# First norm of a hybrid mLSTM / attention / MoE block: the transposes of x go tile of tokens by tile of tokens, and the rotary angles and lambda move into the second projection group

## The chip, the cores and the metric

The kernel runs on one core of a Trainium2 chip. The metric is the device time of one execution in microseconds (us). An engine executes its own instructions in the order in which the program issues them (the schedule is written out by hand, `tc.manual_schedule()`), and waits on semaphores where an operand comes from another engine. The names are those of the profile: PE is TensorE (PEld its weight loads), DVE is VectorE, ACT is ScalarE, POOL is GpSimd, SP is SyncE, which issues most of the DMAs.

## The reference

One decoder block on 512 tokens of width 1024, all in float32:

```python
h = rmsnorm(x, norm1_w) * (1.0 + scale1) + shift1          # scale1, shift1 from c @ w_ada + b_ada
proj = h @ w_in                                             # 5640 columns
(q_m, k_m, v_m, o_m, i_pre, f_pre, q_d, k_d, v_d, g_m, g_d) = split(proj)
qk = silu(causal_conv([q_m, k_m]));  hm = mlstm(...)        # mLSTM branch
qd, kd = partial_rope(rmsnorm(q_d), positions), partial_rope(rmsnorm(k_d), positions)
lam = exp(sum(lam_q1 * lam_k1)) - exp(sum(lam_q2 * lam_k2)) + lam_init
hd = diff_attention(qd, kd, vd, lam)                        # a = p0 - lam * p1
merged = sigmoid(g_m) * (hm @ w_br_m) + sigmoid(g_d) * (hd @ w_br_d)
x = x + gate1 * (merged @ w_out)
x = x + gate2 * hierarchical_moe(rmsnorm(x) * (1 + scale2) + shift2)   # 32 experts, top 2 of one group
```

The change touches the first norm with its modulation (scale1, shift1), the cosines and sines of `partial_rope`, and `lam`.

## The kernel before, in words

**The start.** x comes in four tiles of 128 tokens (`xu`, L115 to L118). For each tile ACT sums the squares (L222), POOL makes 1/rms (L223, L193) and DVE scales the tile in place (L225). The projections need x with the 1024 features on the partitions, so PE transposes 32 blocks of 128x128: `xT(j)` (L306) does feature block j for all four token tiles in one PSUM bank, and ACT (even j) or DVE (odd j) copies the bank back over x in two halves. `mod_rows(fb)` (L278) multiplies c by the part of `w_ada` that belongs to feature blocks 2fb and 2fb+1 (tiles `ada0[fb]`, 2 MB each), ACT copies the row out (L286), `mod_cols(fb)` (L288) turns the row into columns with four small matmuls, and DVE makes the factor and the addend `AB1` from them (L294 to L297). `hT_pair(fb)` (L317) then writes the modulated blocks as a high part (`hTh`, ACT) and a low part (`hTl`, DVE). `warm(n)` issues n matmuls whose result nobody reads.

Between the transposes stand the angles (L354 to L368: DVE, then a Sin on ACT), lambda's exponents (L372 to L374: DVE, then an Exp on ACT), the tables `ropet` (L382) and lambda itself (L384, L385), which one tiny matmul `lamp` (L394) spreads over the partitions and DVE copies to `nlam` (L395). `nlam` and the tables are read much later, by the attention and by `qk_prep`.

**The projections.** `pstream` (L424) runs groups of eight chunks. A chunk is 128 rows of `w_in` by 512 columns: ACT copies them to a high part (L407), DVE or POOL in turn makes the low part (L408), three chunks ahead of use (`LA = 3`), and PE does twelve matmuls of 512 columns (L457 to L459), for each of four banks high by high, high by low, low by high. Behind the chunk's matmuls the program issues what `at(g, k, f)` has put down for group g, chunk k. Then `run` (L478) takes up to two items from the queue `later` and one step of each side generator. In the first group (g = 0) `hT_next` does the modulation of the later feature blocks between the chunks. At its end four banks go out, and each puts a `conv` (L510) into `later`: one ACT instruction (L513), three DVE instructions (L517), and a Silu on ACT (L524) that is inserted behind the next conv. One conv is taken for each chunk, so the four convs fall behind the last chunk of the first group and the first three chunks of the second.

**The rest.** Nine more groups, in whose side generators mLSTM and attention run, then the branch and output projections, the routing, and 16 pairs of experts, whose weights are loaded into buffers as these come free.

The order of SP's DMAs at the start is: x, the four lambda vectors, `ada0[0]`, the first 1 MB of `w_in` (`P0a[0]`), the gate weights, `ada0[1]`, and then halves of `P0a[1]` in turn with `ada0[2]` and `ada0[3]`.

Of the kernel before, what the change touches and what calls it, by code (L numbers as in the profile page):

```python
# [10 lines left out]
F32 = mybir.dt.float32  # L11
# [22 lines left out]
R0, R1 = 3, 0  # L34
RT = (0, 0, 0, 0, 0)
REF = {4: 5, 7: 3, 11: 4}
W0 = (0, 2, 6)
EY, SY = 2, 0
W1 = 6
GF = False  # L40
# [17 lines left out]
def block_kernel(ctx, tc, x, c, positions, w_ada, b_ada, norm1_w, w_in, b_igate, b_fgate, conv_w, conv_b,  # L58
# [16 lines left out]
    def U(name, shape, dt=F32):  # L75
        return up.tile(shape, dt, name=name, tag="u")
# [13 lines left out]
    def ps2(name="ps2"):  # L90
        return ps.tile([128, 2, 512], F32, name=name, tag="s", bufs=1)
# [13 lines left out]
    mrow = dc.tile([24, 128], F32, name="mrow")  # L105
    G.dma_start(posi, positions[0].rearrange("(t p) -> t p", p=128))
    qkw16 = dc.tile([128, 2, 16], F32, name="qkw16")
    for i, w in enumerate((q_norm_w, k_norm_w)):
        G.dma_start(qkw16[:, i], bass.AP(tensor=w.tensor, offset=w.offset, ap=[[0, 128], [1, 16]]))
    cz = amc.rearrange("p a (k f) -> p (a k) f", f=32)  # L110
    S.dma_start(crow[0:8], c[0].rearrange("(j p) -> j p", p=128))
    S.dma_start(crow[8:16], norm1_w[0].rearrange("(j p) -> j p", p=128))
# [2 lines left out]
    xu = [U(f"x{a}", [128, 2, 1024]) for a in range(2)]  # L115
    for t in range(4):
        SP.dma_start(xu[t // 2][:, t % 2], x2[t * 128:(t + 1) * 128])
    for i, w in enumerate((lam_q1, lam_k1, lam_q2, lam_k2)):  # L118
        SP.dma_start(lamt[:, i], w)

    def ada_panel(ch, j):
        t = U("wada", [128, 2048])
# [28 lines left out]

    P0a, P0b = [], []
    load_ada0(0)
    load_unit(P0a, 0, 0, 512)
    SP.dma_start(wif_raw, win[:, 2048:2056].rearrange("(k p) f -> p k f", p=128))
    load_ada0(1)
    P0a.append(U("wp", [128, 4, 512]))
    for i in range(2):
        SP.dma_start(P0a[1][:, 2 * i:2 * i + 2], win[512 + i * 256:768 + i * 256, 0:512].rearrange("(k p) f -> p k f", p=128))
        load_ada0(i + 2)  # L160
    SP.dma_start(rows[0:32], conv_w[0].rearrange("w (j p) -> (w j) p", p=128))
    SP.dma_start(rows[32:40], conv_b[0].rearrange("(j p) -> j p", p=128))
    SP.dma_start(rows[40:44], mlstm_norm_w[0])
# [1 line left out]
    for m in range(2):  # L165
        SP.dma_start(rows[45:46, m * 64:(m + 1) * 64], q_norm_w)
        SP.dma_start(rows[46:47, m * 64:(m + 1) * 64], k_norm_w)

    gb = dc.tile([64, 1], F32, name="gb")
    SP.dma_start(gb[0:4], b_igate[0].rearrange("(h o) -> h o", o=1))  # L170
# [27 lines left out]
    V.memset(onesc, 1.0)  # L198
    onesb = onesc.to_broadcast([128, 128])

    V.tensor_copy(posf, posi)
    post = dc.tile([128, 4], F32, name="post")
    posp = pt("posp", (128, 4))
# [6 lines left out]
    colp = pt("colp", (128, 32))  # L210
    PE.transpose(colp, crow, ident[0:32, 0:32])
    V.tensor_copy(ccols, colp)
    G.memset(cz, 0.0)
    V.tensor_copy(cz[:, :, 0:1], ccol[:, :, None])

# [52 lines left out]
    st = {}  # L268
    AB1 = dc.tile([128, 2, 8], F32, name="AB1")


    def warm(n):
        if n:
            p = ps2("warm")[0:64, 0]
            for _ in range(n):
                PE.matmul(p, wi[:, 0, 0:64], wi[:, 0:4].rearrange("p k f -> p (k f)"), start=True, stop=True)

    def mod_rows(fb):  # L278

        modp = pt("modp") if fb else ps2("modp")[:, 0]  # L280
# [7 lines left out]
    def mod_cols(fb):  # L288

        modp, a_ = pt("modp"), st["ada1"]  # L290
        for i in range(4):
            PE.matmul(modp[:, i:i + 1], a_[:, i * 128:(i + 1) * 128], ones[:, 0:1], start=True, stop=True)
        sl = slice(fb * 2, fb * 2 + 2)
        V.tensor_add(AB1[:, 0, sl], modp[:, 0:2], bcol[:, sl])  # L294
        V.scalar_tensor_tensor(AB1[:, 1, sl], modp[:, 2:4], 1.0, bcol[:, fb * 2 + 8:fb * 2 + 10],
                               op0=ALU.add, op1=ALU.add)
        V.tensor_mul(AB1[:, 1, sl], AB1[:, 1, sl], n1col[:, sl])  # L297

    hTh = [U(f"hTh{a}", [128, 4, 512], F32R) for a in range(2)]
    hTl = [U(f"hTl{a}", [128, 4, 512], F32R) for a in range(2)]  # L300
# [2 lines left out]
    def xcol(j, a):  # L303
        return xu[a][:, :, j * 128:(j + 1) * 128]

    def xT(j):  # L306
        p = pt("xtp") if j in (4, 5) else acc("xtp")
        for t in range(4):
            PE.transpose(p[:, t * 128:(t + 1) * 128], xu[t // 2][:, t % 2, j * 128:(j + 1) * 128], ident)
        for a in range(2):  # L310
            d, q = xcol(j, a), p[:, a * 256:(a + 1) * 256].rearrange("p (t f) -> p t f", t=2)
            if j % 2:
                V.tensor_copy(d, q)
            else:
                S.activation(d, q, AF.Copy)

    def hT_pair(fb):  # L317
        fs = []
# [32 lines left out]
    kf = dc.tile([128, 4, 8], F32, name="kf")  # L351
    MAGIC = 12582912.0
    PI = 3.1415925
    for i in range(8):  # L354
        V.memset(invf[:, i:i + 1], INV_FREQ[i])
    xT(0)
    xT(1)
    V.tensor_mul(ang[:, 1], post[:, :, None].to_broadcast([128, 4, 8]), invf[:, None, :].to_broadcast([128, 4, 8]))
    V.tensor_scalar(kf, ang[:, 1], 1.0 / (2 * math.pi), MAGIC, op0=ALU.mult, op1=ALU.add)
    V.tensor_scalar(kf, kf, -MAGIC, None, op0=ALU.add)  # L360
    for cst in TWO_PI_PARTS:
        V.scalar_tensor_tensor(ang[:, 1], kf, -cst, ang[:, 1], op0=ALU.mult, op1=ALU.add)
    V.tensor_scalar(ang[:, 0], ang[:, 1], math.pi / 2, None, op0=ALU.add)
    V.tensor_scalar(kf, ang[:, 0], math.pi, -2 * math.pi, op0=ALU.is_gt, op1=ALU.mult)
    V.tensor_add(ang[:, 0], ang[:, 0], kf)
    V.tensor_scalar(ang, ang, -PI, PI, op0=ALU.max, op1=ALU.min)
    xT(2)
    S.activation(ang, ang, AF.Sin)  # L368
    xT(3)

    ls = dc.tile([1, 4], F32, name="ls")
    V.tensor_mul(lp, lamt[:, 0:4:2], lamt[:, 1:4:2])  # L372
    V.reduce_sum(ls[:, 0:2], lp, axis=AX.X)
    S.activation(ls[:, 0:2], ls[:, 0:2], AF.Exp)  # L374
    xT(4)
    xT(5)
    rope = []
    for i in range(2):
        tb = dc.tile([128, 4, 4, 8], F32, name=f"ropet{i}")

        for n, (cs, o_) in enumerate(((0, 0), (1, 8), (0, 8), (1, 0))):
            V.tensor_mul(tb[:, n], ang[:, cs], qkw16[:, i, None, o_:o_ + 8].to_broadcast([128, 4, 8]))  # L382
        rope.append(tb)
    V.tensor_sub(ls[:, 2:3], ls[:, 1:2], ls[:, 0:1])  # L384
    V.tensor_scalar(ls[:, 3:4], ls[:, 2:3], -(0.8 - 0.6 * math.exp(-0.3 * 0)), None, op0=ALU.add)  # L385
    warm(W0[0])
    mod_rows(0)
    xT(6)
    xT(7)
    warm(W0[1])  # L390
    mod_cols(0)
    nlam = const.tile([128, 1], F32, name="nlam")
    lamp = acc("lamp")
    PE.matmul(lamp[:, 0:1], ones[0:1, 0:1].to_broadcast([1, 128]), ls[:, 3:4], start=True, stop=True)  # L394
    V.tensor_copy(nlam, lamp[:, 0:1])  # L395
    warm(W0[2])
    pif = ps2("pif")[:, 0]


# [24 lines left out]
    def pstream(groups, ev=None):  # L424
        ev = ev or {}
        chunks = [(g, k) for g in groups for k in range(g.nk)]
        sp_of = {}
        nxt = 0
        for idx, (g, k) in enumerate(chunks):
            if k == 0 and g.pre:  # L430
                g.pre()
            while nxt < len(chunks) and nxt <= idx + LA:
                gg, kk = chunks[nxt]
                sp_of[nxt] = split(gg.w(kk))
                nxt += 1
                if nxt == 1 and g.after:
                    hT_pair(0)
                    wif_split()
            if k == 0:
                g.banks = [acc() for _ in range(4)]  # L440
            wh, wl = sp_of.pop(idx)
            ah, al = g.act(k)
            st, en = (k == 0), (k == g.nk - 1)
            for b in range(4):
                sl = slice(b * 128, (b + 1) * 128)
                if g.kind == "O":
                    hh, tl = b % 2, b // 2
# [1081 lines left out]
```

## Time and profile before

| | us |
|---|---|
| median of three runs | 715.04 (714.26 to 715.83) |
| the profiled execution | 714.36 |
| its span, first to last instruction | 712.6 |
| PE busy | 669.8 (94%) |
| DVE busy | 380.1 (53%) |
| ACT busy | 236.1 (33%) |
| POOL busy | 196.3 (28%) |
| mean granted PE clock | 0.992 |

The rows further down are from the profiled execution; their times count from the first instruction. A row of the timeline gives the start, the duration, engine, line, operation, output and inputs, and how many instructions of one kind are merged in it; in brackets stands how long the engine had been idle before, and what ended that.

### The profile page before, as it was taken

What the parts mean: (1) busy time and instruction counts of PE and PEld (TensorE: products, weight loads), DVE (VectorE), ACT (ScalarE), POOL (GpSimd) and SP (SyncE); (2) the same over time, 40 slices, a digit from 0 to 9 for tenths busy, and PEclk for the clock granted to TensorE, in tenths of its full rate; (3) what the DMA queues carried; (4) which work ended last, traced back from release to release, by engine and by line L of the source; (5) the groups of instructions that cost most, each with busy time, mean ns of one, the idle gap of its engine ahead of it and who ended that gap; (6) DMA issues with size and microseconds to landing.
All of it is one profiled execution on the core that took longest, in us unless ns stands there. A gap on an engine that the chain in (4) does not pass through costs nothing. (4 is left out here: it accounts for less than half of the span.)

```text
span 712.6 us, 11438 instructions
## 1 busy us (share of the span) xinstructions
PE 669.8 (94%) x4464; PEld 493.6 (69%) x4464; DVE 380.1 (53%) x765; ACT 236.1 (33%) x511; POOL 196.3 (28%) x204
## 2 busy tenths in 40 slices
PE   3999999999998999999999999699999999999972
PEld 2668887878777777778867888676667566766630
DVE  4746469866685467763795855763222332233211
ACT  5536582452443455542322234541111111111100
POOL 5213252436552213243253531121111121111100
PEclk9999999999999999999999999999999999999997
DMA  9973069215125011056636984779999999999971
GB/s 300 368 258 150 1 247 402 98 45 187 57 74 178 1 59 60 1 206 221 240 115 237 423 373 178 295 295 357 371 374 379 408 404 378 395 373 401 404 290 21
DMA packets 47386, 171.50 MB, mean 241 GB/s; under 512 B 8009, under 2 KB 16338, under 8 KB 32990
## 3 DMA queue, kind: packets, MB, share of 16 engines
q1 hardware_dynamic: 44510, 165.41, 60.2%
q0 software_dynamic: 2752, 5.28, 3.8%
q8 instruction: 37, 0.61, 0.3%
q14 instruction: 23, 0.19, 0.1%
q10 hardware_dynamic: 64, 0.02, 0.0%
HBM read 164.37 MB, written 10.51 MB: 245 GB/s over the span
## 5 line engine op out<-in xcount | busy, mean ns | idle before, releaser
L408 POOL TENSOR_TENSOR hl<-wp,hl 128x512 fp32r<-128x512 f32 x60 | 85.5, 1426 | 177.0 <-ACT hl L407 160.3
L407 ACT ACTIVATE hl<-wp 128x512 fp32r<-128x512 f32 x120 | 74.3, 627 | 104.0 <-PE acc L458 52.0
L1462 PE MATMUL gu<-we,he 128*64 128x256 f32 x784 | 93.2, 379 | 0.7 <-DMA we<-in_w_gate 0.7
L457 PE MATMUL acc<-hTh,hl 128*128 128x512 f32 x224 | 91.6, 409 | 0.3 <-ACT hTh L324 0.3
L458 PE MATMUL acc<-hTl,hl 128*128 128x512 f32 x224 | 88.4, 395 | 0.2 <-DVE hTl L327 0.2
L459 PE MATMUL acc<-hTh,hl 128*128 128x512 f32 x224 | 88.5, 395 | 0.0
L1462 PEld LDWEIGHTS gu<-we,he 128*64 128x64 f32 x784 | 59.6, 137 | 34.0 <-issue 6.8
L408 DVE TENSOR_TENSOR hl<-wp,hl 128x512 fp32r<-128x512 f32 x60 | 57.7, 963 | 46.8 <-ACT hl L407 46.8
L1308 PE MATMUL gp<-oh,xn 128*128 128x128 f16 x1024 | 64.0, 222 | 2.6 <-DVE oh L1296 1.7
L1308 PEld LDWEIGHTS <-xn 128*128 128x128 f16 x1024 | 60.2, 99 | 8.5 <-issue 5.4
L1469 ACT ACTIVATE sg<-gu 128x256 f32<-128x256 f32 x16 | 6.1, 383 | 173.5 <-PE gu L1462 173.5
L1493 POOL DMA_INDIRECT out<-y,ids x11 | 19.3, 1757 | 141.1 <-DVE y L1488 113.4
L1470 DVE TENSOR_TENSOR sg<-sg,gu 128x256 f32<-128x256 f32 x16 | 6.7, 421 | 94.4 <-ACT sg L1469 94.4
L457 PEld LDWEIGHTS acc<-hTh,hl 128*128 128x128 f32 x224 | 42.1, 188 | 15.4 <-issue 4.7
L461 PE MATMUL acc<-hl,hTh 128*128 128x512 f32 x128 | 52.5, 410 | 0.0
L463 PE MATMUL acc<-hl,hTl 128*128 128x512 f32 x128 | 50.2, 392 | 0.0
L462 PE MATMUL acc<-hl,hTh 128*128 128x512 f32 x128 | 50.1, 392 | 0.0
L1486 PE MATMUL o<-we,sg 128*64 128x512 f32 x192 | 48.3, 598 | 1.1 <-issue 1.1
L459 PEld LDWEIGHTS acc<-hTh,hl 128*128 128x128 f32 x224 | 42.2, 188 | 10.0
L458 PEld LDWEIGHTS acc<-hTl,hl 128*128 128x128 f32 x224 | 42.2, 188 | 9.1 <-DVE hTl L327 0.5
L826 DVE SCALAR_TENSOR_TENSOR wada<-wada,ccols 128x1024 f32<-128x1024 f32 x28 | 40.9, 1485 | 0.6 <-DMA wada<-in_w_ada 0.5
L1326 DVE TENSOR_SCALAR he<-gp,AB 128x128 f32<-128x128 f32 x64 | 21.9, 403 | 20.5 <-PE gp L1308 18.4
(353 smaller groups left out, 1148.9 us busy)
## 6 DMA issues: line engine op xcount, KB each, us to landing
we<-in_w_gate SPq DMA_DIRECT2D x25, 1024.0 KB
we<-in_w_up SPq DMA_DIRECT2D x24, 1024.0 KB
we<-in_w_down SPq DMA_DIRECT2D x24, 1024.0 KB
wp<-in_w_in SPq DMA_DIRECT2D x21, 1024.0 KB
wada<-in_w_ada SPq DMA_DIRECT2D x16, 1024.0 KB
ada<-in_w_ada SPq DMA_DIRECT2D x16, 512.0 KB
wx<-in_w_gate SPq DMA_DIRECT2D x6, 1024.0 KB
wp<-in_w_out SPq DMA_DIRECT2D x4, 1024.0 KB
```

The lines of the kernel that those rows point to most:

```text
L407: S.activation(hi, src, AF.Copy)
L408: (G if LP(n) else V).tensor_sub(lo, src, hi.bitcast(F32))
L457: PE.matmul(g.banks[b], wh[:, sl], ah, start=st, stop=False)
L458: PE.matmul(g.banks[b], wh[:, sl], al, start=False, stop=False)
L459: PE.matmul(g.banks[b], wl[:, sl], ah, start=False, stop=en)
L461: PE.matmul(g.banks[b], ah[:, sl], wh, start=st, stop=False)
L462: PE.matmul(g.banks[b], ah[:, sl], wl, start=False, stop=False)
L463: PE.matmul(g.banks[b], al[:, sl], wh, start=False, stop=en)
L826: V.scalar_tensor_tensor(t0[:, sl], cur[:, sl], ccol[:, j:j + 1], t0[:, sl], op0=ALU.mult, op1=ALU.add)
L1308: PE.matmul(ps_[c_][:, jj * 128:(jj + 1) * 128], part[t // 2][:, t % 2, c_ * 4 + jj], oh[i if st.get("first") else 2][:, t], start=first a ...
L1462: PE.matmul(gu[r, k * 256:(k + 1) * 256], h[:, j, r], wt[key, e][:, j], start=(j == 0), stop=(j == 7), skip_group_check=True)
L1486: PE.matmul(o[r], aT[:, j, r], wt["d", e][:, j, n * 512:(n + 1) * 512], start=(j == 0), stop=(j == 1), skip_group_check=True)
```

## The change

1. `xT` goes over token tiles in the outer loop: for each tile t six transposes, one into each of six banks (feature blocks 0 to 5), and the copies out of the six banks behind all of them. Blocks 6 and 7 follow behind `mod_rows(0)`.
2. The dummy matmuls are counted anew: 4 and 3 ahead of the transposes, 0, 2, 2 and 1 behind the four tiles, 9 behind `mod_cols(0)` (before: 0, 2 and 6 at three places). `warm` is defined further up for this.
3. `mod_cols` makes the columns in the order 2, 0, 3, 1, and `AB1`'s factor with one DVE instruction for each column; the 1 of 1 + scale is added to `bcol` once.
4. The first chunk of the first group does its high by high matmuls for all four banks first, then low by high, then high by low.
5. The angles, the tables, lambda and `lamp` stand in four functions that are issued behind chunks 1 to 4 of the second group (g = 1); the two DMAs of `qkw16` on POOL's queue go with them. `lamp` takes a bank of the tag "t".
6. SP's DMAs: the lambda vectors go behind the small parameter rows; `P0a[0]` comes in halves, the first behind `ada0[0]`, the second behind `ada0[1]`.

```diff
-W0 = (0, 2, 6)
+W0 = (4, 3, 0, 2, 2, 1, 9)
...
-    for i, w in enumerate((lam_q1, lam_k1, lam_q2, lam_k2)):
-        SP.dma_start(lamt[:, i], w)
...
-    load_unit(P0a, 0, 0, 512)
-    SP.dma_start(wif_raw, win[:, 2048:2056].rearrange("(k p) f -> p k f", p=128))
-    load_ada0(1)
...
+    for i in range(4):
+        if i % 2 == 0:
+            P0a.append(U("wp", [128, 4, 512]))
+        SP.dma_start(P0a[i // 2][:, i % 2 * 2:i % 2 * 2 + 2],
+                     win[i * 256:i * 256 + 256, 0:512].rearrange("(k p) f -> p k f", p=128))
+        if i == 0:
+            SP.dma_start(wif_raw, win[:, 2048:2056].rearrange("(k p) f -> p k f", p=128))
+        if i < 3:
+            load_ada0(i + 1)
...
+    warm(W0[0])
...
-        for i in range(4):
+        for i in (2, 0, 3, 1):
...
+        for i in range(2):
+            j = fb * 2 + i
+            V.tensor_scalar(AB1[:, 1, j:j + 1], modp[:, 2 + i:3 + i], bcol[:, j + 8:j + 9], n1col[:, j:j + 1],
+                            op0=ALU.add, op1=ALU.mult)
+            if i == 0:
+                V.tensor_add(AB1[:, 0, sl], modp[:, 0:2], bcol[:, sl])
...
+    def angles():
+        def f0():
+            for i, w in enumerate((q_norm_w, k_norm_w)):
+                G.dma_start(qkw16[:, i], bass.AP(tensor=w.tensor, offset=w.offset, ap=[[0, 128], [1, 16]]))
+            for i in range(8):
+                V.memset(invf[:, i:i + 1], INV_FREQ[i])
+            V.tensor_mul(ang[:, 1], post[:, :, None].to_broadcast([128, 4, 8]),
+                         invf[:, None, :].to_broadcast([128, 4, 8]))
+            V.tensor_scalar(kf, ang[:, 1], 1.0 / (2 * math.pi), MAGIC, op0=ALU.mult, op1=ALU.add)
+            V.tensor_scalar(kf, kf, -MAGIC, None, op0=ALU.add)
+            for cst in TWO_PI_PARTS:
+                V.scalar_tensor_tensor(ang[:, 1], kf, -cst, ang[:, 1], op0=ALU.mult, op1=ALU.add)
+
+        def f1():
+            V.tensor_scalar(ang[:, 0], ang[:, 1], math.pi / 2, None, op0=ALU.add)
+            V.tensor_scalar(kf, ang[:, 0], math.pi, -2 * math.pi, op0=ALU.is_gt, op1=ALU.mult)
+            V.tensor_add(ang[:, 0], ang[:, 0], kf)
+            V.tensor_scalar(ang, ang, -PI, PI, op0=ALU.max, op1=ALU.min)
+            S.activation(ang, ang, AF.Sin)
+
+            V.tensor_mul(lp, lamt[:, 0:4:2], lamt[:, 1:4:2])
+            V.reduce_sum(ls[:, 0:2], lp, axis=AX.X)
+            S.activation(ls[:, 0:2], ls[:, 0:2], AF.Exp)
+
+        def f2():
+            V.tensor_sub(ls[:, 2:3], ls[:, 1:2], ls[:, 0:1])
+            V.tensor_scalar(ls[:, 3:4], ls[:, 2:3], -(0.8 - 0.6 * math.exp(-0.3 * 0)), None, op0=ALU.add)
+
+        def f3():
+            for i in range(2):
+                tb = dc.tile([128, 4, 4, 8], F32, name=f"ropet{i}")
+
+                for n, (cs, o_) in enumerate(((0, 0), (1, 8), (0, 8), (1, 0))):
+                    V.tensor_mul(tb[:, n], ang[:, cs], qkw16[:, i, None, o_:o_ + 8].to_broadcast([128, 4, 8]))
+                rope.append(tb)
+            lamp = pt("lamp")
+            PE.matmul(lamp[:, 0:1], ones[0:1, 0:1].to_broadcast([1, 128]), ls[:, 3:4], start=True, stop=True)
+            V.tensor_copy(nlam, lamp[:, 0:1])
+        return [f0, f1, f2, f3]
+
+    warm(W0[1])
+    xb = {j: acc("xtp") if j < 4 else pt("xtp") for j in range(6)}
+    for t in range(4):
+        xT(range(6), (t,), xb)
+        warm(W0[2 + t])
+    xT_out(range(6), xb)
     mod_rows(0)
-    xT(6)
-    xT(7)
-    warm(W0[1])
+    for j in (6, 7):
+        xb[j] = pt("xtp")
+        xT((j,), range(4), xb)
+    xT_out((6, 7), xb)
     mod_cols(0)
...
+    warm(W0[6])
...
+            if idx == 0:
+
+                for n, (w_, a_) in enumerate(((wh, ah), (wl, ah), (wh, al))):
+                    for b in range(4):
+                        PE.matmul(g.banks[b], w_[:, b * 128:(b + 1) * 128], a_, start=(n == 0), stop=False)
...
+    for i, f in enumerate(angles()):
+        at(1, i + 1, f)
```

## Rows read from the trace of the kernel before

**Rows 1.** The page: PE in the table of busy time, and PE and DMA in the 40 slices of the span.

```profile
PE 669.8 (94%) x4464; PEld 493.6 (69%) x4464; DVE 380.1 (53%) x765; ACT 236.1 (33%) x511; POOL 196.3 (28%) x204
...
PE   3999999999998999999999999699999999999972
...
DMA  9973069215125011056636984779999999999971
```

**Rows 2.** Stretches of the span: the stretch in us, then for each engine its busy time and instructions, the granted PE clock, the DMA engines' busy share, GB/s. The second group up to its chunk 5, and a stretch of the experts.

```profile
60.00:74.13 14.13, 14.13 (x62) 11.43 (x61) 12.53 (x15) 9.42 (x14) 2.99 (x2) 1.00 0.01 5
...
550.00:600.00 50.00, 50.00 (x500) 32.44 (x500) 16.47 (x38) 7.17 (x19) 5.43 (x3) 1.00 1.01 404
```

**Rows 3.** The timeline of the start, from the last tile of x to the end of the first chunk, the instructions on the way of PE alone.

```profile
9.82 1.06 ACT L222 ACTIVATE junk<-x 128x1024 bf16<-128x1024 f32 x1 [1.41 <-DMA x<-in_x]
...
11.91 0.76 DVE L225 TENSOR_SCALAR x<-x,ssq 128x1024 f32<-128x1024 f32 x1 [1.20 <-POOL ssq L193]
...
12.72 3.92 PE L309 MATMUL xtp<-ident,x 128*128 128x128 f32 x21 [1.48 <-DVE x L225]
...
16.58 1.92 PE L283 MATMUL modp<-ada,amc 128*32 128x512 f32 x16
...
18.43 1.09 PE L309 MATMUL xtp<-ident,x 128*128 128x128 f32 x8
...
19.18 0.57 ACT L286 ACTIVATE ada<-modp 128x512 f32<-128x512 f32 x1
...
20.32 0.95 PE L292 MATMUL modp<-ones,ada 128*128 128x1 f32 x8
...
21.51 1.59 PE L276 MATMUL warm<-wi 128*64 128x512 f32 x6
...
22.27 2.08 ACT L324 ACTIVATE hTh<-x,AB 128x256 fp32r<-128x256 f32 x4 [1.48 <-DVE AB L297]
...
23.42 0.51 PE L457 MATMUL acc<-hTh,hl 128*128 128x512 f32 x1 [0.32 <-ACT hTh L324]
...
24.14 0.50 PE L458 MATMUL acc<-hTl,hl 128*128 128x512 f32 x1 [0.22 <-DVE hTl L327]
...
26.57 0.40 PE L459 MATMUL acc<-hTh,hl 128*128 128x512 f32 x1
```

**Rows 4.** Groups of instructions between 8 and 24 us: the copies of the transposed blocks out of PSUM (busy us, mean ns of one).

```profile
L313 DVE COPY x<-xtp 128x256 f32<-128x256 f32 x8 | 3.0, 410 | 1.3 <-PE xtp L309 1.3
L315 ACT ACTIVATE x<-xtp 128x256 f32<-128x256 f32 x8 | 2.6, 368 | 3.3 <-PE xtp L309 3.3
```

**Rows 5.** The DMAs of the start: the issue of `ada0[0]` on SP's queue, and stretches of the span with their GB/s (last column).

```profile
6.17 4.00 SPq L147 DMA_DIRECT2D ada<-in_w_ada  x4
```

```profile
0.00:10.00 10.00, 1.34 (x4) 0.65 (x4) 2.36 (x10) 4.91 (x8) 7.67 (x20) 1.00 0.81 257
10.00:20.00 10.00, 7.48 (x47) 5.33 (x48) 7.12 (x39) 6.57 (x15) 1.69 (x7) 1.00 1.09 354
...
7.00:8.00 1.00, 0.19 (x2) 0.06 (x1) 0.81 (x4) 0.89 (x3) 0.68 (x2) 1.00 0.74 204
```

**Rows 6.** The timeline of PE from 12.7 to 15.3 us: the first twelve of the 21 transposes.

```profile
12.72 2.82 PE L309 MATMUL xtp<-ident,x 128*128 128x128 f32 x12 [1.48 <-DVE x L225]
```

**Rows 7.** The timeline of DVE and ACT in the second group (`conv` is L513 on ACT and L517 on DVE, its Silu is L524, the split of `w_in` is L407 and L408).

```profile
61.32 2.32 DVE L517 SCALAR_TENSOR_TENSOR cy<-craw,cols,cy 128x511 f32<-128x511 f32 x3 [5.08 <-ACT cy L513]
63.56 0.68 DVE L408 TENSOR_TENSOR hl<-wp,hl 128x512 fp32r<-128x512 f32 x1
64.16 5.59 DVE L517 SCALAR_TENSOR_TENSOR cy<-craw,cols,cy 128x511 f32<-128x511 f32 x6
69.67 1.79 DVE L408 TENSOR_TENSOR hl<-wp,hl 128x512 fp32r<-128x512 f32 x1
```

```profile
67.43 1.53 DVE L517 SCALAR_TENSOR_TENSOR cy<-craw,cols,cy 128x511 f32<-128x511 f32 x2
```

```profile
63.72 1.28 ACT L524 ACT_TABLE_LOAD   x1
...
67.61 0.63 ACT L524 ACTIVATE qTm<-cy 128x512 f32<-128x512 f32 x1 [0.74 <-DVE cy L517]
68.15 0.80 ACT L513 ACTIVATE cy<-craw,cols 128x512 f32<-128x512 f32 x1
```

**Rows 8.** The timeline of PE where chunk 5 of the second group begins.

```profile
74.22 0.40 PE L457 MATMUL acc<-hTh,hl 128*128 128x512 f32 x1
```

**Rows 9.** The timeline of the start again: the angles and lambda on DVE and ACT, which the change moves.

```profile
12.62 0.17 DVE L355 MEMSET invf<- 128x1 f32 x8
...
14.76 0.18 DVE L358 TENSOR_TENSOR ang<-post,invf 128x32 f32<-128x32 f32 x1
...
16.09 0.18 DVE L363 TENSOR_SCALAR ang<-ang 128x32 f32<-128x32 f32 x1
...
16.97 0.26 ACT L368 ACTIVATE ang<-ang 128x64 f32<-128x64 f32 x1
17.25 1.28 ACT L374 ACT_TABLE_LOAD   x1
...
18.54 0.20 ACT L374 ACTIVATE ls<-ls 1x2 f32<-1x2 f32 x1
...
19.50 0.14 DVE L384 TENSOR_TENSOR ls<-ls 1x1 f32<-1x1 f32 x1
...
19.68 0.14 DVE L385 TENSOR_SCALAR ls<-ls 1x1 f32<-1x1 f32 x1
```

**Rows 10.** A wait of PE in the routing, and the stretches around it.

```profile
454.47 0.18 PE L1277 MATMUL rkp<-rmaskb,before 128*128 128x32 bf16 x1 [2.72 <-DVE rmaskb L1268]
```

```profile
454.47:456.00 1.53, 0.68 (x11) 0.58 (x11) 1.34 (x7) 0.00 (x0) 0.00 (x0) 1.00 1.01 428
456.00:459.40 3.40, 3.40 (x35) 3.40 (x33) 3.16 (x9) 0.00 (x0) 0.00 (x0) 0.50 0.77 318
```

More of the change, by code (lines that the diff above doesn't have):

```diff
@@ L107, in block_kernel @@
     qkw16 = dc.tile([128, 2, 16], F32, name="qkw16")
-    for i, w in enumerate((q_norm_w, k_norm_w)):
-        G.dma_start(qkw16[:, i], bass.AP(tensor=w.tensor, offset=w.offset, ap=[[0, 128], [1, 16]]))
     cz = amc.rearrange("p a (k f) -> p (a k) f", f=32)
@@ L153, in block_kernel @@
     load_ada0(0)
-    load_unit(P0a, 0, 0, 512)
-    SP.dma_start(wif_raw, win[:, 2048:2056].rearrange("(k p) f -> p k f", p=128))
-    load_ada0(1)
[L157 to L160, printed above, removed]
+    for i in range(4):
[7 more added lines that the diff above has]
+            load_ada0(i + 1)
     SP.dma_start(rows[0:32], conv_w[0].rearrange("w (j p) -> (w j) p", p=128))
@@ L167, in block_kernel @@
         SP.dma_start(rows[46:47, m * 64:(m + 1) * 64], k_norm_w)
+    for i, w in enumerate((lam_q1, lam_k1, lam_q2, lam_k2)):
+        SP.dma_start(lamt[:, i], w)
     gb = dc.tile([64, 1], F32, name="gb")
@@ L199, in block_kernel, with warm @@
     onesb = onesc.to_broadcast([128, 128])
+    def warm(n):
+        if n:
+            p = ps2("warm")[0:64, 0]
+            for _ in range(n):
+                PE.matmul(p, wi[:, 0, 0:64], wi[:, 0:4].rearrange("p k f -> p (k f)"), start=True, stop=True)
+    warm(W0[0])
     V.tensor_copy(posf, posi)
@@ L212, in block_kernel @@
     V.tensor_copy(ccols, colp)
+    V.tensor_scalar(bcol[:, 8:16], bcol[:, 8:16], 1.0, None, op0=ALU.add)
     G.memset(cz, 0.0)
@@ L269, in block_kernel @@
     AB1 = dc.tile([128, 2, 8], F32, name="AB1")
[L272 to L276, printed above, removed]
     def mod_rows(fb):
@@ L290, in mod_cols @@
         modp, a_ = pt("modp"), st["ada1"]
-        for i in range(4):
+        for i in (2, 0, 3, 1):
             PE.matmul(modp[:, i:i + 1], a_[:, i * 128:(i + 1) * 128], ones[:, 0:1], start=True, stop=True)
         sl = slice(fb * 2, fb * 2 + 2)
[L294 to L297, printed above, removed]
+        for i in range(2):
[4 more added lines that the diff above has]
+                V.tensor_add(AB1[:, 0, sl], modp[:, 0:2], bcol[:, sl])
     hTh = [U(f"hTh{a}", [128, 4, 512], F32R) for a in range(2)]
@@ L304, in xcol, with xT, xT_out @@
         return xu[a][:, :, j * 128:(j + 1) * 128]
[L306 to L315, printed above, removed]
+    def xT(js, ts, banks):
+        for t in ts:
+            for j in js:
+                PE.transpose(banks[j][:, t * 128:(t + 1) * 128], xu[t // 2][:, t % 2, j * 128:(j + 1) * 128], ident)
+    def xT_out(js, banks):
+        for j in js:
+            for a in range(2):
+                d, q = xcol(j, a), banks[j][:, a * 256:(a + 1) * 256].rearrange("p (t f) -> p t f", t=2)
+                if j % 2:
+                    V.tensor_copy(d, q)
+                else:
+                    S.activation(d, q, AF.Copy)
     def hT_pair(fb):
@@ L353, in block_kernel @@
     PI = 3.1415925
[L354 to L369, printed above, removed]
-    ls = dc.tile([1, 4], F32, name="ls")
-    V.tensor_mul(lp, lamt[:, 0:4:2], lamt[:, 1:4:2])
-    V.reduce_sum(ls[:, 0:2], lp, axis=AX.X)
-    S.activation(ls[:, 0:2], ls[:, 0:2], AF.Exp)
@@ L375, in block_kernel @@
-    xT(4)
-    xT(5)
-    rope = []
[L378 to L386, printed above, removed]
+    ls = dc.tile([1, 4], F32, name="ls")
@@ new lines, in block_kernel @@
+    nlam = const.tile([128, 1], F32, name="nlam")
+    rope = []
+    def angles():
[32 more added lines that the diff above has]
+        return [f0, f1, f2, f3]
@@ L387, in block_kernel @@
+    warm(W0[1])
[4 more added lines that the diff above has]
+    xT_out(range(6), xb)
     mod_rows(0)
-    xT(6)
-    xT(7)
-    warm(W0[1])
+    for j in (6, 7):
+        xb[j] = pt("xtp")
+        xT((j,), range(4), xb)
+    xT_out((6, 7), xb)
     mod_cols(0)
-    nlam = const.tile([128, 1], F32, name="nlam")
-    lamp = acc("lamp")
-    PE.matmul(lamp[:, 0:1], ones[0:1, 0:1].to_broadcast([1, 128]), ls[:, 3:4], start=True, stop=True)
@@ L395, in block_kernel @@
-    V.tensor_copy(nlam, lamp[:, 0:1])
-    warm(W0[2])
+    warm(W0[6])
     pif = ps2("pif")[:, 0]
@@ L443, in pstream @@
             st, en = (k == 0), (k == g.nk - 1)
+            if idx == 0:
+                for n, (w_, a_) in enumerate(((wh, ah), (wl, ah), (wh, al))):
+                    for b in range(4):
+                        PE.matmul(g.banks[b], w_[:, b * 128:(b + 1) * 128], a_, start=(n == 0), stop=False)
             for b in range(4):
+                if idx == 0:
+                    break
                 sl = slice(b * 128, (b + 1) * 128)
```

## The prediction

> **What bounds the kernel now.** I read the page's busy table and slices first: PE is busy for 94% of the span, and from the third slice on its digit is 9 nearly everywhere, while DMA is full only at both ends [rows 1]. The stretches say the same: PE fills all of the second group and all of a stretch of the experts, where the DMA engines are full too (404 GB/s) [rows 2]. The experts' loads start when PE lets go of a buffer, so a microsecond that PE gains or loses earlier moves them along and stays in the total. So two questions decide: when does PE begin its first chunk (23.42 us [rows 3]), and does anything make it wait later that didn't before?
>
> **The start.** Before, the last tile of x is scaled by 11.91 + 0.76 = 12.67 us. Then stand, all on PE's way: the remaining 21 transposes of blocks 0 to 5 to 16.58, `mod_rows` 1.92, eight transposes 1.09, `mod_cols` from 20.32 for 0.95, DVE's three instructions until ACT begins `hTh` at 22.27, and the first matmul 1.15 later [rows 3]. The twelve first transposes took 2.82, some 0.22 each [rows 6]; the last eight took 1.09, some 0.12 each [rows 3]. So PE runs at the lower of its two levels (1.2 GHz) at first; the clock column shows 1.00 in that stretch [rows 5] and can't be used there.
>
> After the change only 6 transposes need the last tile. In between PE has the 12 transposes of tiles 1 and 2 and four dummies. At 0.22, and 0.46 for a dummy (an estimate: twice the 0.23 that six in 1.59 come to when the tail of the last is taken off [rows 3]), this work, begun at about 9.7, ends at about 14.2, and with the six and one dummy more at 16.0; at the higher level (2.4 GHz) from about 12.5 on it is 14.3. I take 14.4, as seven dummies ahead of the transposes should bring the clock up sooner. `mod_rows(0)` needs 4.19 MB landed (x and `ada0[0]`). Before, 2.57 MB came in the first 10 us and 354 GB/s after, which is 14.6; the rate dips to 204 GB/s at 7 to 8 us, while SP issues `ada0[0]` only from 6.17 to 10.17 [rows 5]. Without the lambda vectors ahead this issue comes earlier, so the weights are there by 13.7 to 14.6, and only the second half of `mod_rows` can be touched. Thus:
> - `mod_rows` 14.4 to 16.3; eight transposes to 17.4. ACT has done six copies at 0.37 by then (13.9 to 16.1 [rows 4]), then the row's copy 0.57 [rows 3], then block 6 to about 17.9, which frees the bank that `mod_cols` writes.
> - `mod_cols` 17.9 to 18.85, DVE about 0.25 (before about 1.0 up to ACT's start; the order 2, 0, 3, 1 leaves two of the instructions behind the last matmul), `hTh` 1.15: PE could begin at 20.25.
> - The nine dummies take 9 x 0.23 from 18.85 and so hold PE until 20.9, where six were covered before. I take 20.5 for the first matmul: 2.9 gained. Bounds: 19.9 (the clock up early, 3.5 gained) and 22.0 (clock down and weights late, 1.4).
> - The first chunk took 23.42 to 26.80 [rows 3], twelve matmuls at 0.23 take 2.8; high by low comes last now, so its wait goes: 0.6 (0.3 to 0.6).
>
> In all 3.5 us (1.7 to 4.1). The split of `P0a[0]` and the other order of DMAs I cost at nothing: the second half lands at about 22 and is wanted by chunk 2, behind `mod_rows(1)`, at about 27; cover gone, it would cost up to 1. The move of the small DMAs on POOL's queue is hidden by POOL's idle time in the second group (2.99 busy of 14.13 [rows 2]). The extra DVE instruction on `bcol` (0.15) lies ahead of the scaling of tile 0, which isn't late.
>
> **The second group.** Here I count in the times of the trace of before, as PE's chunks, the convs and the splits keep their distances. DVE has no idle time from 61.32 to past 71 [rows 7]; it is busy 12.53 of 14.13 [rows 2]. The order on each engine, with the four pieces put in, is:
> - DVE: conv 0, split, conv 1, **f0**, conv 2, split, **f1**, conv 3, **f2**, split, **f3**.
> - ACT: ..., **Sin, Exp**, Silu of conv 1, conv 3's scaling, the split of chunk 6, ...
> - PE: chunk 4, **`lamp`**, chunk 5.
>
> `lamp` reads what f2 writes, and PE comes to it at 74.2 [rows 8]. The chain to f2, step by step:
> - conv 1 is over when conv 2 begins, at 67.43 [rows 7];
> - f0: eight memsets 0.17, then 14.76 to 16.09 in the start: 1.5 [rows 9], to 68.9;
> - conv 2, 67.43 to 69.67: 2.24; split 0.68 (1.79 when POOL works beside it) [rows 7]: to 71.9;
> - f1: from 16.09 to Sin at 16.97: 0.88; Sin 0.26 [rows 9]: to 73.0 (lambda's product and sum run beside it);
> - the table load for Exp 1.28, Exp 0.20 [rows 9]: to 74.5;
> - Silu was last in force before Sin, so its table is loaded again, 1.28; Silu 0.55 and conv 3's scaling 0.80 [rows 7]: to 77.1;
> - conv 3 on DVE 2.3, as conv 0 took 2.32 [rows 7]: to 79.5; f2's two instructions 0.32 [rows 9]: 79.8.
>
> So PE, which has chunk 5 and everything after queued behind `lamp`, waits from 74.2 to 79.8: 5.6 us. The split of chunk 6, which is late as well (ACT gets to it at 77.1, POOL is done at some 79), is hidden behind that wait; without it, it would cost 2 at most. Bounds: 3.5 (POOL and ACT out of DVE's way, each step at its shortest) and 7.
>
> A wait like this one has a price behind it. In the routing PE waited 2.72 us, did little for another 1.5, and then the granted clock was 0.50 for 3.4 us, with PE busy throughout [rows 10]: 1.7 lost. I add 1.2 for the wait of 5.6 (0 to 1.7), as part of the low stretch may fall into the wait itself.
>
> **The sum.** -3.5 + 5.6 + 1.2 = +3.3. The profiled execution took 714.36 (span 712.6), so 717.7 for its like; the median of before lies 0.7 above that execution, which makes 718.4.
>
> The row of the table load bears on a rule: Exp starts at 18.54, right behind the load of 1.28 that began at 17.25 [rows 9]. The Trainium skill's page "ScalarE: Activation LUTs", section "What ACT_TABLE_LOAD costs", puts a drain of about 1380 ns to each switch, some 2.66 us in all, and its section "Table sets: the hidden batching unit" asks to do all of one set before switching, which f1 between two Silus does not. The trace shows no such drain. By the page, Exp and the second Silu load would each cost 1.4 more on the chain to f2, and the sum would be 721.2, an estimate from that page.
>
> **Rivals.**
> - *The wait on f2 is met in time* (not slower). Place: `lamp` behind chunk 4; it decides whether f2 ends before 74.2. Then the 5.6 and 1.2 fall away, and the start alone counts: 715.04 - 3.5 = 711.5. For it: f0 to f3 are short by themselves, about 4 us of DVE, and DVE stands idle for 5.08 ahead of conv 0. Against: that idle time ends with conv 0's scaling on ACT, which waits for PE's banks; f2 stands behind conv 3, and conv 3 behind two table loads on ACT.
> - *The two cancel.* A wait of 3.5 without loss of clock against a start of 3.5: 715.0.
> - *The start gives little.* Clock down until 16, weights late, nine dummies in the way: 1.7 gained, the wait at 5.6 and the clock at 1.7: 715.04 + 5.6 = 720.6.
> - *Longer switches* on ACT (two of 1.4 more, by the nearest row no more than the 1.28 of a load again): 715.04 + 3.3 + 2.6 = 720.9.
>
> **How the numbers follow.** A change under 0.2% (1.4 us) can't be told from none here. The likeliest, 718.4 (its own range 716.5 to 720.0): 0.52. Met in time, 711.5: 0.20. Cancel: 0.12. Little at the start: 0.11. Longer switches: 0.05. Faster is the second case with a part of the third, 0.22; within 0.2% the rest of the third and a little of the first, 0.12; slower 0.66. For 8 in 10 the range must take in part of the second case: 711.6 to 721.0.
>
> **What would show it.** Right: a wait of PE at `lamp` of 4 to 7 us, ended by DVE's f2, with three table loads on ACT ahead of it, and a stretch of clock 0.5 behind it; the first chunk at 20 to 21 us, its matmuls without a gap. Wrong: `lamp` without a wait (then it is faster), a first chunk behind 22, or another wait in the second group.

## The result, and the profile after

The changed kernel takes 721.22 us (median of five runs, 720.09 to 722.37); the kernel before takes 715.04 in the runs beside it. The ratio is 1.0081, with a 95% interval of 1.0056 to 1.0106: slower, by about 6 us. The profiled execution took 721.22, and its span is 719.5, 6.9 longer than before.

PE in the page's slices and the granted clock, to hold against [rows 1]:

```profile
PE   7999699999998999999998999889999999999972
PEclk9999899999999999999999999799999999999997
```

PE is busier in the first slice (7 instead of 3) and has a 6 in the fifth, 72 to 90 us, where the granted clock drops too.

The timeline of the start (one row for each stage on PE's way), which answers to [rows 3]:

```profile
11.23 0.76 DVE L236 TENSOR_SCALAR x<-x,ssq 128x1024 f32<-128x1024 f32 x1 [0.72 <-POOL ssq L195]
...
12.12 0.82 PE L315 MATMUL xtp<-ident,x 128*128 128x128 f32 x6
...
14.52 1.06 PE L287 MATMUL modp<-ada,amc 128*32 128x512 f32 x8 [0.19 <-DMA ada<-in_w_ada]
...
15.64 0.60 ACT L290 ACTIVATE ada<-modp 128x512 f32<-128x512 f32 x1 [1.45 <-PE modp L287]
...
16.92 1.05 PE L296 MATMUL modp<-ones,ada 128*128 128x1 f32 x8 [0.31 <-ACT x L324]
...
17.83 2.26 PE L208 MATMUL warm<-wi 128*64 128x512 f32 x9
...
18.46 2.08 ACT L333 ACTIVATE hTh<-x,AB 128x256 fp32r<-128x256 f32 x4 [1.07 <-DVE AB L303]
...
19.93 2.02 PE L471 MATMUL acc<-hTh,hl 128*128 128x512 f32 x8
...
22.81 1.92 PE L287 MATMUL modp<-ada,amc 128*32 128x512 f32 x16
```

Only six transposes stand behind the last tile of x (0.82, where 21 took 3.92), the first chunk begins at 19.93 instead of 23.42, and the work behind it at 22.81; before, that stood at 26.90, so this execution is 4.1 us ahead there.

PE's waits between 20 and 130 us (total, times, longest), and the timeline of the second group on ACT, DVE, POOL and PE from f1 on:

```profile
PE lamp L403 <- DVE ls L393: 7.1, 1, 7.1
PE amp L598 <- DVE am L592: 1.0, 1, 1.0
```

```profile
68.49 0.26 ACT L385 ACTIVATE ang<-ang 128x64 f32<-128x64 f32 x1 [5.73 <-DVE ang L384]
68.75 1.28 ACT L389 ACT_TABLE_LOAD   x1
70.05 0.20 ACT L389 ACTIVATE ls<-ls 1x2 f32<-1x2 f32 x1
70.25 1.28 ACT L554 ACT_TABLE_LOAD   x1
71.55 0.63 ACT L554 ACTIVATE qTm<-cy 128x512 f32<-128x512 f32 x1
72.08 0.80 ACT L543 ACTIVATE cy<-craw,cols 128x512 f32<-128x512 f32 x1
```

```profile
72.91 4.09 DVE L547 SCALAR_TENSOR_TENSOR cy<-craw,cols,cy 128x511 f32<-128x511 f32 x3 [3.96 <-ACT cy L543]
76.92 0.14 DVE L392 TENSOR_TENSOR ls<-ls 1x1 f32<-1x1 f32 x1
77.10 0.14 DVE L393 TENSOR_SCALAR ls<-ls 1x1 f32<-1x1 f32 x1
```

```profile
73.48 1.30 POOL L431 TENSOR_TENSOR hl<-wp,hl 128x512 fp32r<-128x512 f32 x1 [11.00 <-ACT hl L430]
75.04 1.41 POOL L431 TENSOR_TENSOR hl<-wp,hl 128x512 fp32r<-128x512 f32 x1 [0.25 <-ACT hl L430]
```

```profile
77.39 0.55 PE L403 MATMUL lamp<-ls,ones 1*128 1x1 f32 x2 [7.12 <-DVE ls L393]
77.87 0.80 PE L487 MATMUL acc<-hTh,hl 128*128 128x512 f32 x1
78.46 0.63 PE L488 MATMUL acc<-hTl,hl 128*128 128x512 f32 x1
```

Read from PE back: `lamp` is released by DVE's L393, the second instruction of f2, and stood 7.12 idle for it. f2 ran directly behind conv 3, which DVE had awaited for 3.96 us; conv 3 came behind ACT's scaling at 72.08, that behind a Silu, a table load, Exp, another table load, and Sin, for whose operand ACT had stood idle for 5.73. Note that DVE was idle between Exp's end at 70.25 and 72.91: f2's operands were there and DVE was free, but conv 3 stood ahead in its queue.

The granted clock in the wait and behind it, and in a later stretch (columns as in [rows 2]):

```profile
70.27:77.39 7.12, 0.00 (x2) 0.03 (x1) 4.37 (x6) 4.97 (x8) 2.72 (x2) 0.83 0.00 0
77.39:81.85 4.46, 4.46 (x11) 3.63 (x12) 1.36 (x10) 0.33 (x1) 0.00 (x0) 0.50 0.01 4
...
225.20:228.60 3.40, 3.40 (x9) 2.65 (x8) 0.69 (x1) 1.18 (x2) 0.00 (x0) 0.50 0.98 307
```

How far the changed kernel is ahead or behind, by the start of the same instruction of PE in the two traces:

| instruction | before | after | after - before |
|---|---|---|---|
| last gate matmul of the first group | 60.02 | 55.91 | -4.1 |
| first matmul of the third group | 82.58 | 88.11 | +5.5 |
| `amp` | 114.00 | 119.95 | +5.9 |
| last `hnT` of mLSTM | 230.91 | 238.35 | +7.4 |
| `mrp` | 387.29 | 394.15 | +6.9 |
| last output matmul of an expert | 699.67 | 706.66 | +7.0 |

So the second group alone takes 9.6 us more: 7.1 of wait, 0.5 for `lamp` itself, and 1.9 for the nine matmuls behind it, at about 0.43 instead of 0.23. The rest is small: 0.4 more wait at `amp`, 1.5 in a second stretch of low clock at 225 us, and 0.5 given back at `mrp`, which waits for a DMA.

### The profile page after: what moved, and what is told of

Its sections match the earlier page's. It is cut to its first block, busy times and chain, and to the rows that moved or that the text cites. A ratio compares the mean times of both kernels' runs of the same rounds, so it can differ in the third digit from the quotient of the medians.

```text
span 719.5 us, 11467 instructions
## 1 busy us (share of the span) xinstructions
PE 678.1 (94%) x4477; PEld 498.2 (69%) x4477; DVE 379.9 (53%) x766; ACT 236.6 (33%) x511; POOL 196.3 (27%) x204
## 5 line engine op out<-in xcount | busy, mean ns | idle before, releaser
L431 POOL TENSOR_TENSOR hl<-wp,hl 128x512 fp32r<-128x512 f32 x60 | 84.2, 1404 | 183.7 <-ACT hl L430 169.3
L430 ACT ACTIVATE hl<-wp 128x512 fp32r<-128x512 f32 x120 | 74.4, 628 | 109.6 <-PE acc L488 52.3
L431 DVE TENSOR_TENSOR hl<-wp,hl 128x512 fp32r<-128x512 f32 x60 | 54.3, 905 | 53.2 <-ACT hl L430 53.1
```

Source lines behind the costliest of these rows:

```text
L430: S.activation(hi, src, AF.Copy)
L431: (G if LP(n) else V).tensor_sub(lo, src, hi.bitcast(F32))
```

## The experiments

The theory: PE's wait at `lamp` comes from f2's place in DVE's queue and from what stands ahead of it on ACT, and has nothing to do with the new start, which is a gain. Its rivals: the table loads cost wherever f2 stands; the pieces hurt only in this group; the wait needs the earlier start.

**f2 ahead of conv 3.**

```diff
             S.activation(ls[:, 0:2], ls[:, 0:2], AF.Exp)
+            V.tensor_sub(ls[:, 2:3], ls[:, 1:2], ls[:, 0:1])
+            V.tensor_scalar(ls[:, 3:4], ls[:, 2:3], -(0.8 - 0.6 * math.exp(-0.3 * 0)), None, op0=ALU.add)

         def f2():
-            V.tensor_sub(ls[:, 2:3], ls[:, 1:2], ls[:, 0:1])
-            V.tensor_scalar(ls[:, 3:4], ls[:, 2:3], -(0.8 - 0.6 * math.exp(-0.3 * 0)), None, op0=ALU.add)
+            pass
```

> The changed kernel with lambda's two DVE instructions (f2) taken from behind conv 3 to right behind Exp, ahead of conv 3 on DVE; nothing else. If the wait of PE at lamp comes from f2's place in DVE's queue behind conv 3, f2 is over some 0.4 us after Exp (70.25 in the changed kernel's trace), PE waits at lamp for about 0.5 instead of 7.1, then about 1.5 at chunk 6, whose low half (POOL) is late since ACT's split stands behind the table loads; the clock stays up: 721.2 - 7.1 + 2.0 - 1.7 = 714.4 (713 to 716). If the table loads on ACT are what costs (they stand ahead of every split), moving f2 only moves the wait to chunk 6: a wait of 4 or more there, and 718 or more.

It takes 712.40 against 715.11 (ratio 0.9955, 0.9937 to 0.9974): two instructions of 0.14 us each, put 6 us earlier into a queue, make a slower kernel into a faster one. PE's waits in the second group:

```profile
PE lamp L404 <- DVE ls L391: 0.5, 1, 0.5
PE acc L490 <- POOL hl L432: 0.4, 1, 0.4
```

The wait at `lamp` is the expected 0.5. Chunk 6 waits only 0.4 where 1.5 was expected, which is some of why the time is 2 below the forecast. All three table loads of the stretch are still there (for the first Silu, for Exp, and for Silu again), so they aren't the price; what stood between Exp and f2 on DVE was.

**The pieces in the third group.**

```diff
-        at(1, i + 1, f)
+        at(2, i + 4, f)
```

> The changed kernel with the four pieces behind chunks 4 to 7 of the third group instead of chunks 1 to 4 of the second; nothing else. If the start's gain (4.1 us at the beginning of the second group) is real and the pieces cost only where convs fill DVE, no wait at lamp: 715.0 - 4.1 = 710.9 (710 to 713). If the pieces cost wherever they stand, since PE takes lamp in order and ACT changes tables, a wait of 2 or more at lamp or at a chunk of the third group, and 714 to 720.

A miss: 721.19 (1.0082, 1.0060 to 1.0103), no faster than the changed kernel. PE waits 9.58 at `lamp`:

```profile
110.35 0.55 PE L403 MATMUL lamp<-ls,ones 1*128 1x1 f32 x2 [9.58 <-DVE ls L393]
```

The timeline of ACT and then DVE in that group:

```profile
98.31 0.26 ACT L385 ACTIVATE ang<-ang 128x64 f32<-128x64 f32 x1 [5.15 <-DVE ang L384]
98.59 1.28 ACT L389 ACT_TABLE_LOAD   x1
99.88 0.20 ACT L389 ACTIVATE ls<-ls 1x2 f32<-1x2 f32 x1
100.10 1.28 ACT L554 ACT_TABLE_LOAD   x1
...
102.70 1.28 ACT L577 ACT_TABLE_LOAD   x1
...
104.64 1.28 ACT L578 ACT_TABLE_LOAD   x1
...
106.58 1.15 ACT L430 ACTIVATE hl<-wp 128x512 fp32r<-128x512 f32 x2
```

```profile
107.25 1.65 DVE L431 TENSOR_TENSOR hl<-wp,hl 128x512 fp32r<-128x512 f32 x1 [8.47 <-ACT hl L430]
108.81 1.21 DVE L392 TENSOR_TENSOR ls<-ls 1x1 f32<-1x1 f32 x1
```

f2 stands here behind DVE's half of a split (L431), and that waits for ACT's half (L430), which comes behind Exp, the last Silu and the gates' Abs, Exp and Ln (L576 to L578): four table loads from Sin on. Exp was over at 100.08. It is the same fault in another place: f2 behind something on DVE that waits for ACT behind Exp. I had looked only for room on DVE and at the convs, and not at what the gates do on ACT in that group.

**The wait filled with dummies.**

```diff
-            lamp = pt("lamp")
+            lamp, wp_ = pt("lamp"), pt("warm")[0:64]
+            for _ in range(30):
+                PE.matmul(wp_, wi[:, 0, 0:64], wi[:, 0:4].rearrange("p k f -> p (k f)"), start=True, stop=True)
```

> The changed kernel with 30 dummy matmuls of 512 columns (7.0 us at 0.232) on PE ahead of lamp, in the stretch in which it waits. If the low clock behind the wait is a cost by itself, the wait of 7.1 is filled, lamp starts at the same time, chunk 5 runs at 0.232 a matmul instead of 0.425, and the time falls by 1.7 to 719.5 (718.5 to 720.5). If the clock has no part in it, 721.2 as before.

719.26 against 715.11 (1.0061, 1.0040 to 1.0083), with ten runs between 717.24 and 722.73. The trace shows the mechanism: `lamp` is late by the same amount, but the chunk behind it runs at 0.23 a matmul from its second on.

```profile
70.90 7.08 PE L404 MATMUL warm<-wi 128*64 128x512 f32 x30
78.16 0.38 PE L405 MATMUL lamp<-ls,ones 1*128 1x1 f32 x2 [0.18 <-DVE ls L393]
78.47 0.50 PE L489 MATMUL acc<-hTh,hl 128*128 128x512 f32 x1
78.80 0.39 PE L490 MATMUL acc<-hTl,hl 128*128 128x512 f32 x1
79.03 0.40 PE L491 MATMUL acc<-hTh,hl 128*128 128x512 f32 x1
```

So the low clock behind the wait is a price of its own. By the times, its size is open: the median fell as expected, but the interval overlaps the changed kernel's (1.0056 to 1.0106). By the trace it is the 1.9 of the nine matmuls.

**The kernel before with the pieces alone moved.** The diff is part 5 of the change put on the kernel before.

> The kernel before with part 5 alone: the four pieces behind chunks 1 to 4 of the second group, with the two POOL DMAs; the old order of transposes, dummies, chunk 0 and SP's DMAs. If the wait at lamp comes from these pieces and not from the earlier start, PE waits 6 to 7.5 there, the clock falls after it, and the start gains under 1 from the work taken out: 715.0 + 9.6 - 0.5 = 724 (722 to 725.5). If the wait needs the earlier start (PE ahead of DVE and ACT by more), it is shorter than 4 and the time 716 to 720.

723.24 against 715.11 (1.0116, 1.0091 to 1.0140), as expected: the wait is 7.1 here too, and so needs nothing of the new start.

```profile
PE lamp L392 <- DVE ls L382: 7.1, 1, 7.1
```

The first chunk begins at 23.56, not earlier than the 23.42 of before. PE gets to the 21 transposes 0.6 earlier here, but they and `mod_rows` run at the slow spacing for longer (the transposes at 0.23 to the last; 4.74 and 2.38, against 3.92 and 1.92 in [rows 3]), and that eats the lead:

```profile
12.08 4.74 PE L307 MATMUL xtp<-ident,x 128*128 128x128 f32 x21 [1.00 <-DVE x L223]
16.75 2.38 PE L281 MATMUL modp<-ada,amc 128*32 128x512 f32 x16
```

So taking the pieces out of the old start gained nothing in this execution; what it would gain with the clock up as early as before isn't shown.

**The new transposes with the pieces left in the start.**

```diff
     xT_out(range(6), xb)
+    fa = angles()
+    for f in fa[:3]:
+        f()
     mod_rows(0)
...
     mod_cols(0)
+    fa[3]()
     warm(W0[6])
...
-    for i, f in enumerate(angles()):
-        at(1, i + 1, f)
```

> The changed kernel with the pieces put back into the start: f0, f1 and f2 behind the copies out of the six banks, ahead of mod_rows(0), f3 behind mod_cols(0); the new transposes, dummies, chunk 0 and DMAs stay. If the start's gain needs the pieces out of the way, ACT copies mod_rows' row only behind Sin and Exp with their table loads, about 3 later than at 15.64, and the first chunk begins at about 23 (19.93 in the changed kernel, 23.42 before); with no wait in the second group about 715 (714 to 716.5). If the transposes tile by tile are the gain by themselves, the first chunk begins by 21 and the time is 712 or less.

A miss by a wide margin: 740.78 against 716.11 (1.0348). The wait is not the one that I had in mind. DVE's waits between 15 and 60 us, longest first:

```profile
DVE M L387 <- DMA M<-in_lam_k: 22.3, 1, 22.3
```

I had left the lambda vectors' DMAs where the change puts them, behind the parameter rows, and there they land at about 40 us. So part 6 of the change can't stand without part 5. The same kernel with these four DMAs behind `ada0[0]`:

```diff
     load_ada0(0)
+    for i, w in enumerate((lam_q1, lam_k1, lam_q2, lam_k2)):
+        SP.dma_start(lamt[:, i], w)
...
-    for i, w in enumerate((lam_q1, lam_k1, lam_q2, lam_k2)):
-        SP.dma_start(lamt[:, i], w)
```

> The fifth experiment's kernel (the pieces in the start, new transposes) with the four lambda vectors' DMAs taken from behind the parameter rows, where they landed at about 40 us, to right behind ada0[0]; nothing else. If the fifth's 25 us were the wait of DVE, and of ACT and PE behind it, for these vectors, it goes, and what is left is the price of the pieces in the start: ACT copies mod_rows' row behind Sin, a table load and Exp, at about 20 instead of 15.64, the first chunk begins at 23.5 to 24.5 (23.42 before), and the time is 715.5 (714 to 717). If another cause held the fifth up, 720 or more.

716.13 against 715.33 (1.0021, 1.0003 to 1.0038). On ACT the row's copy (L290) is at 18.56 instead of 15.64, behind Sin, a table load and Exp (Sin's own load, at 14.10, is over before Sin's operand comes). The first chunk begins at 23.80:

```profile
14.10 1.28 ACT L385 ACT_TABLE_LOAD   x1
16.88 0.26 ACT L385 ACTIVATE ang<-ang 128x64 f32<-128x64 f32 x1 [1.50 <-DVE ang L384]
...
17.16 1.28 ACT L389 ACT_TABLE_LOAD   x1
18.45 0.20 ACT L389 ACTIVATE ls<-ls 1x2 f32<-1x2 f32 x1
18.56 0.57 ACT L290 ACTIVATE ada<-modp 128x512 f32<-128x512 f32 x1
```

With the fourth experiment this makes a square: the first chunk begins at 23.42 (old transposes, pieces in the start), 23.56 (old, pieces moved), 23.80 (new, pieces in the start) and 19.93 (new, pieces moved). In these four profiles neither half gains alone, and both together do. The new start was tried with the pieces ahead of the row's copy on ACT, as in the kernel before, and not with them behind it.

**The pieces apart, `lamp` far behind f2.**

```diff
-            S.activation(ang, ang, AF.Sin)
-
             V.tensor_mul(lp, lamt[:, 0:4:2], lamt[:, 1:4:2])
             V.reduce_sum(ls[:, 0:2], lp, axis=AX.X)
-            S.activation(ls[:, 0:2], ls[:, 0:2], AF.Exp)
+
+        def f1b():
+            S.activation(ang, ang, AF.Sin)
+            S.activation(ls[:, 0:2], ls[:, 0:2], AF.Exp)
...
                 rope.append(tb)
+
+        def f4():
             lamp = pt("lamp")
...
-        return [f0, f1, f2, f3]
+        return [(1, 1, f0), (1, 3, f1), (1, 6, f1b), (1, 7, f2), (1, 7, f3), (2, 3, f4)]
...
-    for i, f in enumerate(angles()):
-        at(1, i + 1, f)
+    for g, k, f in angles():
+        at(g, k, f)
```

> The changed kernel with the pieces apart: f0 behind chunk 1 of the second group, f1's DVE part behind chunk 3, Sin and Exp behind chunk 6 (the Silus of the first group's convs are over), f2 and the tables behind chunk 7, lamp alone behind chunk 3 of the third group. If the waits come from ACT and DVE standing in order behind Sin and Exp, and from lamp's place too close behind them, no wait at lamp and none at chunk 6: the 0.5 and 0.4 left in the first experiment fall away, 712.4 - 0.9 = 711.5 (710.5 to 712.5). If the table loads cost wherever they stand, a wait of 1 or more at a chunk of the second or third group, and 713 or more.

710.58 against 716.11 (0.9927, 0.9913 to 0.9940): the fastest here, and clear of the kernel before by 5.5 us in the same runs. PE has no idle time from 60 to 100 us:

```profile
60.00:100.00 40.00, 40.00 (x175) 32.31 (x174) 28.20 (x60) 29.89 (x45) 15.56 (x13) 1.00 0.25 88
```

The table loads are as many as in the changed kernel and hold nothing up that PE waits for in this stretch.

**No dummies around the transposes** (on the first experiment's kernel):

```diff
-W0 = (4, 3, 0, 2, 2, 1, 9)
+W0 = (0, 0, 0, 0, 0, 0, 9)
```

> The first experiment's kernel (f2 early) without the twelve dummies around the transposes (the nine behind mod_cols stay); nothing else. If the dummies bring the clock up sooner (some 10 us in the changed kernel, some 16 before, by the spacing of the transposes) and that is worth time, the transposes run at 0.21 up to the last tile and the first chunk begins 0.5 to 1.5 later: 712.4 + 1 = 713.4 (712.8 to 714.2). If the landing of the weights for mod_rows sets the start anyway, the first chunk begins at the same time within 0.3: 712.4.

712.83 against 716.11 (0.9957, 0.9943 to 0.9971); the first experiment had 0.9955. The 24 transposes run as one row of 0.2 each, and are done before the second half of the weights is there:

```profile
8.09 4.87 PE L315 MATMUL xtp<-ident,x 128*128 128x128 f32 x24 [1.21 <-DVE x L236]
...
14.92 1.07 PE L287 MATMUL modp<-ada,amc 128*32 128x512 f32 x8 [0.96 <-DMA ada<-in_w_ada]
```

The first chunk begins at 20.34, with the dummies at 20.45. The weights' landing sets the start, and the twelve dummies are worth nothing that these runs can show.

**The old order in the first chunk** (on the first experiment's kernel):

```diff
-            if idx == 0:
+            if False:

                 for n, (w_, a_) in enumerate(((wh, ah), (wl, ah), (wh, al))):
...
-                if idx == 0:
-                    break
```

> The first experiment's kernel (f2 early) with the old order of the matmuls in the first chunk (bank by bank); a look at the trace alone. If the new order takes the wait for the low part out, the chunk has a gap of about 0.5 again between its first and second matmul, and takes 3.4 from its first matmul to the next work instead of 2.9. If the low part is in time anyway, 2.8 and no gap.

This is from one execution. From the first matmul to the next work the chunk takes 3.16 (20.63 to 23.79), and 2.88 with the new order (20.45 to 23.33), so 0.3 is what the new order gives here, half of what was expected; the second matmul comes 0.39 behind the first instead of 0.23, not 0.72 as in [rows 3].

## Why the prediction was right, and where it was off

The direction and the mechanism came out as forecast: a gain at the start, and a wait of PE at `lamp` with a stretch of low clock behind it. The time, 718.4, was 2.8 too low: 721.22 lies above the 716.5 to 720.0 of the likeliest case, and 0.2 above the upper end of the whole range. Step by step:

- *The start, 3.5 gained.* Measured 4.1: the first chunk at 19.93 instead of 20.5, and 0.6 in the first chunk, of which the eighth experiment gives 0.3 to the new order. The 4.1 is this execution's: in the four experiments with the whole of the new start (the first three and the sixth) the first chunk begins at 19.98 to 20.68, and PE is 3.3 to 4.1 ahead at the last gate matmul. A part isn't of the change: the last tile of x was scaled by 11.99 instead of 12.67, and the fourth experiment, with the old order of DMAs, has it by 12.02. That the weights for `mod_rows` set the pace was right: PE waits for their second half in the changed kernel (0.2) and in six of the nine experiments (0.5 to 1.0). The dummies do bring the clock up sooner, as forecast (six transposes in 0.82 behind them, against 0.2 each throughout without them), but as the weights come later still, it was worth nothing that shows.
- *That PE's gain stays in the total* held: the offsets in the table change only where PE waits or its clock falls.
- *The chain to f2, 5.6 of wait.* Its order was right in every link: Sin without a load, then loads for Exp and for Silu. In the forecast Silu of conv 1 starts at 75.8 in times of before, which is 71.7 with the 4.1 taken off; measured 71.55. The term that was mis-sized is conv 3's 2.3: it took 4.09, while two of POOL's splits, held up behind the same table loads, ran beside it (73.48 to 76.45). The size follows that overlap in all profiles: of the four convs at the end of the first group, those without a split of POOL beside them take 2.31 or 2.32, those with one 3.3 (conv 1, and conv 2 in the sixth experiment alone), those with two 4.1 to 4.2 (conv 3 in the changed kernel and five experiments). The forecast had a price of that meeting in its hands (a split of 0.68 that took 1.79 with POOL beside it), but took conv 3 at the time of conv 0. With 4.1 the wait would have been 7.4; it was 7.1.
- *The clock behind the wait, 1.2.* Measured 1.9 for the nine matmuls. The second stretch, at 225 us, isn't in the sum: PE's wait at `sT`, 1.55 to 1.66 in every profile here, was followed by such a stretch in the changed kernel and in four experiments (f2 early, no dummies, the old chunk, and the pieces in the start with the lambda vectors early), and by none before and in the others. What decides that stays open.
- *The rival that the wait is met in time* is what the first and the sixth experiments built, and they took 712.4 and 710.6, near its 711.5.
- *The sum.* Against +3.3 the profiled execution has +6.9: 0.6 more gained at the start, 1.5 more wait and 0.7 more clock behind it, and four terms that the sum had at nothing, `lamp` itself (0.5), `amp` (0.4), the second stretch (1.5) and `mrp` (-0.5). The rival *the start gives little* has 720.6, nearer to the measured time, but for another reason than the runs show: the start gained 3.3 to 4.1, not 1.7.
- *The drain*, which the Trainium skill's page "ScalarE: Activation LUTs" adds to each table load in its section "What ACT_TABLE_LOAD costs", isn't to be seen on either side of a load: Exp's load begins where Sin ends (68.49 + 0.26), Exp begins 0.02 behind the end of its load (68.75 + 1.28 against 70.05), and the load for Silu and Silu likewise. So it is luck that the 721.2 estimated with that drain meets the measured time; the missing microseconds are those listed above.

## What to carry to other kernels

Work that is moved off one path takes its order on every engine along: look at what the moved result stands behind on the engine that makes it, and at what stands behind the instruction that reads it. A `lamp` of 0.5 us, whose result is first read 171 us later (at 249.57 in the changed kernel), held PE for 7.1, as it was issued close behind its producer; put such readers far behind, and issue a small producer right behind its own operand rather than behind work that waits for a longer chain. Two edits in one place that gain nothing alone may gain together: measure them together before dropping one.

## What the runs showed of the hardware that wasn't expected

- Sin behind Silu needed no table load in the changed kernel: ACT's row at 68.49 has none ahead of it, where Sin in the start has one of 1.28 (the row at 14.10 in the last experiment on the start).
- DVE's conv took 4.09 instead of 2.31 for the same three instructions while POOL did two splits of its own. With the pieces in the third group (the second experiment), two DVE instructions that take 0.18 and 0.19 in the changed kernel took 1.16 and 1.04 beside POOL's gate instructions.
- The wait of 7.1 on PE is followed by a granted clock of 0.50 for 4.5 us of its work (77.39 to 81.85); where the same stretch is filled with 30 dummy matmuls, the clock stays at 1.00.
